# Differential and local attention: products with the values for pairs of query blocks

## The chip, the core and the metric

The kernel runs on one NeuronCore of a Trainium2 chip. The metric is the device time of one execution, in microseconds (us), from runs without the profiler; a further, profiled execution gives the trace from which all rows below are taken. TensorE multiplies matrices (in the profile PE; the loading of its stationary operand is PEld), VectorE is DVE, ScalarE is ACT, GpSimd is POOL, and SyncE (SP) issues most loads.

## The reference

Two transformer-like blocks follow each other on a sequence of 1024 positions and width 1024, all in float32. The change touches the attention of the second block. Cut to what matters:

```python
# local (sliding window) attention: 8 heads, a block of 128 queries sees its own and the block before
scores = q_block @ [k_prev, k_own].T * d**-0.5 - slope * delta          # masked, window 128
p      = softmax([scores, sink])[..., :-1]
out_a  = p @ [v_prev, v_own]                                            # 256 keys -> 64 columns
# differential attention: 4 heads of two maps, causal, a block of 128 queries sees all keys before it
p      = softmax(q_m @ k_m.T * d**-0.5 - slope * delta)                 # m = 0, 1
out_d  = (p_0 - lam * p_1) @ v                                          # up to 1024 keys -> 128 columns
out_d  = rmsnorm(out_d, subln_g) * 0.8                                  # over the 128 columns of a head
merged = sigmoid(ga) * (out_a @ w_branch_swa) + sigmoid(gd) * (out_d @ w_branch_diff)
x      = x + gate1 * (merged @ w_out)
```

## The kernel before

The sequence is worked on in two halves of 512 columns. Projections (`proj`, tile `pj`) keep activations transposed and split every operand into a high and a low part, so that a product is three TensorE rows of 512 columns (`wh` with both parts of the activation, `wl` with the high part). They are emitted in a fixed order by `run_...()` calls. Everything else is a generator, a side task: attention units, norms, sums. The class `Sched` holds an estimated clock for each engine and decides, before each projection row, which side task's next rows are emitted ahead of it; `Sched.note` has the estimated duration of each operation. So the order on each engine is settled when the kernel is built. Where a projection needs what a side task makes, `sch.until(...)` emits side tasks' rows alone until a flag is set. The body is built twice, the first time to learn when tiles come free.

`swa` (L1233) is the local attention: a unit `(t, n)` has two heads and one block of 128 queries; scores go into one bank (`z`), the softmax is in tile `p`, `turn(p, 4)` transposes its four 128x128 blocks on TensorE (`tr`) and copies them on ScalarE into `pT` (`aT` in the trace), and the products with the values go into a bank `o` of four query blocks. Two heads write partitions 0 to 63 and 64 to 127 of it.

`diff` (L1314) is the differential attention. A unit `(h, i)` is a head and a block of queries with `n = i + 1` blocks of keys. `softmax` runs for both maps in turn: scores `z`, one or two VectorE passes that add the bias and take the maximum, the exponential on ScalarE, a scaling on VectorE. Then `p0` is turned, and `n` products of one 128x128 block of `v` (`vp`, stationary) with 128 columns of `aT` are summed in `o`. When a head's four blocks are done, `sub_norm` squares, sums (`sm`), spreads the factor (`rb`), scales, and splits the result into the activation `od` that the branch projection `job_br` reads. All of these products are plain float32; each stands in the trace as two PE records and two PEld records.

`crew` keeps at most `width` units alive (2 in the second half, `PACE`). `fetched` issues the loads of the next head on SP as soon as `room(tiles + KEEP)` finds that many of the 34 large tiles free (`N4`, `in_use`); `work` asks `room` for its own large tiles. A block with more than 512 keys needs three large ones (two maps, one turned), a shorter one none.

The second half of `diff` is to be done when `run_br1` (the branch projection) starts:

```python
        run_g1()
        run_up0()
        sch.until(lambda: ("attn2", 1) in flags)
        run_br1()
```

Of the kernel before, what the change touches and what calls it, by code (L numbers as in the profile page):

```python
# [18 lines left out]
HT = 512  # L19
# [38 lines left out]
class Sched:  # L58
# [94 lines left out]
    def note(self, eng, op, out, args, extra=0.0):  # L153
        ready = self.ready
        names = [a.tensor.name for a in args]
        self.seq += 1
        start = max([self.clk[eng]] + [ready.get(n, 0.0) for n in names])
        o = out.tensor.name
        n = out.free_size()
        lat = 0.1  # L160
        if eng == "pe":
            start = max(start, self.fresh.pop(o, 0.0))
            if op == "transpose":
                d = 0.113 if self.t > 30.0 else 0.213
            elif args[0].dtype == F32R:
                d = n / 2400 if n >= 256 else n / 600
            elif args[0].dtype == BF16:
                d = n / 2400
            elif n == 1:
                d = 0.2 if self.t > 30.0 else 0.37  # L170
            else:
                d = n / 600 if args[0].free_size() == 128 else n / 1070
            d += 0.0026
        elif eng == "act":
            d = n / 1400 + 0.155 + extra
        elif eng == "dve":
            fast = op in ("tensor_scalar", "tensor_copy") and all(a.space == out.space != bass.MemoryType.PSUM
                                                                  for a in args)
            d = n / (1920 if fast else 960) + 0.06
            if op == "reciprocal":  # L180
                d += n / 192
        else:
            d = 1.05 if eng == "pool" else 0.55
            nbytes = n * out.shape[0] * 4
            t = max(self.clk["dma"], start + d) + nbytes / 360e3
            self.clk["dma"] = t
            lat = t + 1.8 - start - d
        self.clk[eng] = start + d
        for nme in names + [o]:
            self.last[nme] = self.seq, max(start + d + lat, self.last.get(nme, (0, 0.0))[1])  # L190
        ready[o] = max(ready.get(o, 0.0), start + d + lat) if eng != "pe" else start + d + lat
        if eng != "pe":
            for nme in names:
                b = self.in_bank.get(nme)
                if b is not None:
                    b[0] = max(b[0] or 0.0, start + d)
# [68 lines left out]
def tile_body(  # L265
# [14 lines left out]
    sch = Sched()  # L280
# [3 lines left out]
    mm = ten.matmul  # L284
# [12 lines left out]
    out = out[0]  # L297
# [10 lines left out]
    def free(n=1):  # L308

        in_use[0] -= n  # L310

    def room(n, hold=0):

        while in_use[0] + n > N4:
            yield 0.4
        in_use[0] += hold

    def big(shape, dt=F32, name="b", held=False):
        in_use[0] += not held
        return s4.tile([128] + shape, dt, nm(name))  # L320

    def sml(w=HT, dt=F32, name="s"):
        return s2.tile([128, w], dt, nm(name))
# [4 lines left out]
    def bank(name="ps"):  # L328
        return sch.new_bank(lambda n: pp.tile([128, HT], F32, tag=f"bk{n}", name=nm(name)))
# [679 lines left out]
    def turn(src, n):  # L1009

        dst = wide(n * 128, name="aT", held=True)
        for b0 in range(0, n, 4):
            b1 = min(n, b0 + 4)
            yield from sch.a_bank()
            ps = bank("tr")
            for b in range(b0, b1):
                ten.transpose(out=ps[:, (b - b0) * 128:(b - b0 + 1) * 128],
                              in_=src[:, b * 128:(b + 1) * 128], identity=ident)
            sca.copy(out=dst[:, b0 * 128:b1 * 128], in_=ps[:, 0:(b1 - b0) * 128])
        yield dst  # L1020
        return dst

    def fetched(loads, keys, need, fetch, tiles, ahead=1):

        for n, key in enumerate(keys):
            while (need(key) not in flags) or (n > ahead and keys[n - ahead - 1] not in loads["done"]):
                yield 0.5
            yield from room(tiles + (KEEP if n else 0))
            loads[key] = fetch(key)
# [203 lines left out]
    def swa(live, half, width, rho):  # L1233
# [15 lines left out]
        def work(t, n):  # L1249
# [32 lines left out]
                vec.tensor_scalar(out=p[:, 256 * h:256 * h + 256], in0=p[:, 256 * h:256 * h + 256],  # L1282
                                  scalar1=l[:, h:h + 1], scalar2=None, op0=ALU.mult)
            yield p
            pT = yield from turn(p, 4)
            if t not in st:
                yield from sch.a_bank()
            if t not in st:
                st[t] = [bank("o"), 0]
            po = st[t][0]  # L1290
            g = t // 2
            blocks = [(0, n - 1), (1, n)] if n else [(0, 0)]
            for a, (b, kb) in enumerate(blocks):
                for h in range(2):
                    mm(po[64 * h:64 * h + 64, (n % 4) * 128:(n % 4 + 1) * 128],
                       lhsT=vas[0][:, kb, 64 * g:64 * g + 64],
                       rhs=pT[:, (2 * h + b) * 128:(2 * h + b + 1) * 128],
                       start=a == 0, stop=a == len(blocks) - 1)
            st[t][1] += 1
            if st[t][1] == 4:  # L1300
                del loads[t], st[t]
                loads["done"].add(t)
# [11 lines left out]
    def diff(live, half, width, rho):  # L1314
# [43 lines left out]
        def work(h, i):  # L1358
            yield from arrived(loads, h)
            n = i + 1  # L1360
            w = n * 128
            yield from room(3 * (w > HT), 3 * (w > HT))
            p0, l0 = yield from softmax(h, i, 0)
            vec.tensor_scalar(out=p0[:, 0:w], in0=p0[:, 0:w], scalar1=l0[:, 0:1], scalar2=None, op0=ALU.mult)
            p1, l1 = yield from softmax(h, i, 1)
            vec.scalar_tensor_tensor(out=p0[:, 0:w], in0=p1[:, 0:w], scalar=l1[:, 0:1], in1=p0[:, 0:w],
                                     op0=ALU.mult, op1=ALU.add)
            free(w > HT)
            fr = st.setdefault(("f", h), set())
            fr.add(i)  # L1370
            if len(fr) == 4:
                del loads[h]
                loads["done"].add(h)
                free(3 + half)
            yield p0
            aT = yield from turn(p0, n)
            free(w > HT)
            if h not in st:
                yield from sch.a_bank()
            if h not in st:  # L1380
                st[h] = [bank("o"), 0]
            po = st[h][0]
            vt = vts[h]
            yield vt
            for kb in range(n):
                mm(po[:, (i % 4) * 128:(i % 4 + 1) * 128], lhsT=vt[:, kb * 128:(kb + 1) * 128],
                   rhs=aT[:, kb * 128:(kb + 1) * 128], start=kb == 0, stop=kb == n - 1)
            free(w > HT)
            st[h][1] += 1
            if st[h][1] == 4:  # L1390
                del st[h], vts[h]
                free(half)
                o = sml(name="od")
                sca.copy(out=o, in_=po)
                sq = sml(name="sq")
                act(out=sq, in_=po, func=ACTF.Square)
                sch.spawn(sub_norm(h, o, sq))
# [936 lines left out]
```

## Time and profile before

| | |
|---|---|
| median of 3 runs | 2580.68 us (2580.65 to 2581.55) |
| the profiled execution's own time | 2582.41 us, its span 2580.6 us |
| TensorE (PE) busy | 2505.5 us, 97% of the span |
| its granted clock, mean over the span | 0.991 of full speed |
| VectorE, ScalarE, GpSimd busy | 69%, 49%, 19% of the span |

The span is the time between the first and the last instruction. Busy time counts records that overlap once. The granted clock is the share of TensorE's full speed (2.4 GHz) that the throttle allowed; it has two levels, full and half.

### The profile page before, as it was taken

To read this page: it belongs to the slowest core of one execution; us is meant where nothing else is said; L and a number is where in the kernel's file an instruction comes from. 1 tells how busy PE (TensorE), PEld (TensorE's weight loads), DVE (VectorE), ACT (ScalarE), POOL (GpSimd) and SP (SyncE) were. 2 spreads that over 40 slices of the span, in tenths; PEclk is the share of its full clock that TensorE was granted. 3 is DMA by queue.
4 is the path that set the end of the run, shared out by engine and by line. 5 is a ranking of instruction groups with operands and counts; after the bars stand their busy time and mean duration, and the time that the engine had idled before them with its cause. 6 is when DMAs were issued, how large, how long until landed. Compare 5 with 4: busy or idle time off the path is not lost.

```text
span 2580.6 us, 38805 instructions
## 1 busy us (share of the span) xinstructions
PE 2505.5 (97%) x13215; PEld 2057.5 (80%) x13215; DVE 1792.8 (69%) x3245; ACT 1255.7 (49%) x2529; POOL 490.0 (19%) x894
## 2 busy tenths in 40 slices
PE   7999999989999899998999999999999899999998
PEld 6888888879877677787888887888888678788887
DVE  7866666777697788986765556774666876677555
ACT  5311112555455677677664353564634634345442
POOL 0012112312101002331211321222222222221000
PEclk9999999999999999999999999999999999999999
DMA  9867869857897665775876978977886987978764
GB/s 283 264 190 201 203 214 280 235 185 249 279 274 222 204 163 157 221 192 140 250 217 160 262 209 261 260 226 220 200 237 217 237 225 235 238 225 252 226 201 130
DMA packets 541726, 570.43 MB, mean 221 GB/s; under 512 B 32910, under 2 KB 410008, under 8 KB 541528
## 3 DMA queue, kind: packets, MB, share of 16 engines
q1 hardware_dynamic: 482644, 381.99, 50.3%
q0 software_dynamic: 56528, 181.75, 25.3%
q10 hardware_dynamic: 2356, 4.21, 0.4%
q8 instruction: 104, 1.70, 0.3%
q14 instruction: 94, 0.77, 0.1%
HBM read 466.90 MB, written 186.91 MB: 253 GB/s over the span
## 4 chain that ended last, share of the span: by engine, by line
PE 65%; DVE 5%; DMA 3%; ACT 2%; issue 2%; SPq 0%; POOL 0%; DVEq 0%; ACTq 0%; POOLq 0%
PE pj L249 53%; PE o L249 4%; PE z L249 4%; PE tr L250 3%; DVE om L250 2%; PE pv L249 1%; DMA wr<-sg_d2g 1%; DVE be L250 1%; DVE wl L250 1%; DMA wr<-in_b_w_out_dram 1%; DVE ob L250 1%; DVE act L250 0%; DVE fa L250 0%; ACT om L250 0%; ACT be L250 0%
## 5 line engine op out<-in xcount | busy, mean ns | idle before, releaser
L249 PE MATMUL pj<-act,wh 128*128 128x512 f32 (+1 forms) x5680 | 1783.0, 395 | 26.2 <-DVE act L250 16.8
L249 PEld LDWEIGHTS pj<-act,wh 128*128 128x128 f32 x5680 | 1046.2, 189 | 256.8 <-DVE act L250 22.9
L249 PE MATMUL pj<-act,wl 128*128 128x512 f32 (+1 forms) x2840 | 1113.7, 392 | 0.0
L249 PEld LDWEIGHTS pj<-act,wl 128*128 128x128 f32 x2840 | 536.2, 189 | 123.1 <-DVE wl L250 1.3
L250 DVE TENSOR_TENSOR wl<-wr,wh 128x512 fp32r<-128x512 f32 x714 | 476.4, 679 | 169.7 <-ACT wh L250 156.2
L250 ACT CAST wh<-wr 128x512 fp32r<-128x512 f32 x714 | 425.8, 617 | 177.6 <-PE pj L249 41.8
L250 POOL COPY paced<-wl 128x1 f32<-128x1 f32 x256 | 114.7, 448 | 881.6 <-DVE wl L250 840.9
L250 ACT COPY aT<-tr 128x512 f32<-128x512 f32 (+3 forms) x272 | 128.7, 501 | 162.0 <-PE tr L250 159.6
L249 PE MATMUL z<-kd,qs 128*128 128x512 f32 (+2 forms) x704 | 166.4, 350 | 1.7 <-DVE o L250 0.7
L250 DVE SCALAR_TENSOR_TENSOR acc<-mw,silu_c,acc 128x512 f32<-128x512 f32 x196 | 146.5, 748 | 2.7 <-DMA mw<-in_a_mod_w_dram 0.3
L249 PEld LDWEIGHTS z<-kd,qs 128*128 128x128 f32 x704 | 113.7, 190 | 19.4 <-issue 7.2
L250 DVE TENSOR_TENSOR_SCAN om<-om,begin 128x640 f32<-128x640 f32 (+3 forms) x64 | 120.6, 1885 | 10.2 <-ACT om L250 10.2
L249 PEld LDWEIGHTS o<-aT,vp 128*64 128x64 f32 (+2 forms) x1440 | 99.9, 149 | 22.8 <-issue 14.5
L249 PE MATMUL o<-aT,vp 128*64 128x128 f32 (+2 forms) x1440 | 116.3, 280 | 0.4 <-ACT aT L250 0.4
L250 ACT COPY u<-pj 128x512 f32<-128x512 f32 x46 | 27.0, 588 | 157.8 <-PE pj L249 80.1
L250 ACT ACTIVATE p<-p,t 128x256 f32<-128x256 f32 (+7 forms) x128 | 81.3, 636 | 20.7 <-DVE t L250 20.5
L250 ACT ACTIVATE sq<-xn 128x512 f32<-128x512 f32 x48 | 30.6, 637 | 110.6 <-DVE xn L250 110.5
L250 ACT ACTIVATE om<-z 128x384 f32<-128x384 f32 (+2 forms) x128 | 69.3, 542 | 22.6 <-PE z L249 19.0
L249 PE MATMUL pj<-wh,act 128*128 128x256 f32 x448 | 79.9, 281 | 0.0
L250 PE MATMUL tr<-ident,be 128*128 128x128 f32 x416 | 61.1, 283 | 18.1 <-DVE be L250 17.7
L250 PEld LDWEIGHTS tr<-ident,be 128*128 128x128 f32 x416 | 47.3, 143 | 32.4 <-DVE be L250 20.7
L250 DVE TENSOR_TENSOR be<-be,om 128x639 f32<-128x639 f32 (+3 forms) x64 | 66.2, 1034 | 6.7 <-ACT sq L250 0.5
(252 smaller groups left out, 2757.5 us busy)
## 6 DMA issues: line engine op xcount, KB each, us to landing
wr<-in_w_in_dram SPq DMA_DIRECT2D x136, 256.0 KB
mw<-in_w_ada_dram SPq DMA_DIRECT2D x96, 256.0 KB
wr<-in_a_w_in_dram SPq DMA_DIRECT2D x80, 256.0 KB
al<-dn_d SPq DMA_DIRECT2D x77, 256.0 KB
wr<-in_w_up_dram SPq DMA_DIRECT2D x66, 256.0 KB
sw_d<-in_w_down_dram POOLq DMA_DIRECT2D x48, 352.0 KB, 5.0
wr<-in_b_w_qz_dram SPq DMA_DIRECT2D x64, 256.0 KB
qs<-q_d SPq DMA_DIRECT2D x64, 256.0 KB
```

The costliest lines, as they stand in the source:

```text
L249: return f(out, *value, **kw)
L250: return f(out=out, **kw)
```

## The change

A unit no longer multiplies by itself. In `diff`, blocks `i0` and `i0 + 1` share turned tiles in which 256 columns stand for each block of keys, 128 of either query block (`pair_new`, `turn_pair`). The unit that ends second multiplies for both: each key block of `v` is loaded once and 256 columns pass it; the last key block, which only the odd query block sees, gets 128. The large tiles of a pair (one or two) are asked for by the even unit and given back after the products. In `swa`, the pair's turned blocks share one large tile `pT`; the key block that both query blocks see gets 256 columns, its two neighbours 128. The planner's estimate for float32 products is changed too: before, 128 columns at 600 per us (1070 with 64 stationary columns); now, 1100 per us and at least 0.213 us (2200 and 0.108).

```diff
             elif n == 1:
                 d = 0.2 if self.t > 30.0 else 0.37
             else:
-                d = n / 600 if args[0].free_size() == 128 else n / 1070
+                d = max(n / 1100, 0.213) if args[0].free_size() == 128 else max(n / 2200, 0.108)
             d += 0.0026
         elif eng == "act":
             d = n / 1400 + 0.155 + extra
@@ -1019,6 +1019,30 @@
             sca.copy(out=dst[:, b0 * 128:b1 * 128], in_=ps[:, 0:(b1 - b0) * 128])
         yield dst
         return dst
+
+    def pair_tiles(i):
+
+        return (i % 8) // 2 if i < 4 else 2
+
+    def pair_new(i):
+        return [sml(name="aT")] if i == 0 else [big([2 * HT], name="aT", held=True) for _ in range(pair_tiles(i))]
+
+    def pair_block(tiles, kb, j):
+
+        return tiles[kb // 4][:, kb % 4 * 256 + 128 * j:kb % 4 * 256 + 256]
+
+    def turn_pair(src, n, tiles, j):
+
+        for b0 in range(0, n, 4):
+            b1 = min(n, b0 + 4)
+            yield from sch.a_bank()
+            ps = bank("tr")
+            for b in range(b0, b1):
+                ten.transpose(out=ps[:, (b - b0) * 128:(b - b0 + 1) * 128],
+                              in_=src[:, b * 128:(b + 1) * 128], identity=ident)
+            dst = tiles[b0 // 4].rearrange("p (k j q) -> p k j q", j=2, q=128)
+            sca.copy(out=dst[:, 0:b1 - b0, j, :], in_=ps[:, 0:(b1 - b0) * 128].rearrange("p (k q) -> p k q", q=128))
+        yield tiles
 
     def fetched(loads, keys, need, fetch, tiles, ahead=1):
 
@@ -1282,21 +1306,37 @@
                 vec.tensor_scalar(out=p[:, 256 * h:256 * h + 256], in0=p[:, 256 * h:256 * h + 256],
                                   scalar1=l[:, h:h + 1], scalar2=None, op0=ALU.mult)
             yield p
-            pT = yield from turn(p, 4)
+            n0, j = n & ~1, n % 2
+            if (t, n0) not in st:
+                yield from room(1)
+            if (t, n0) not in st:
+                st[t, n0] = [big([2, HT], name="aT"), []]
+            pT, done = st[t, n0]
+            yield from sch.a_bank()
+            ps = bank("tr")
+            for b in range(4):
+                ten.transpose(out=ps[:, b * 128:(b + 1) * 128], in_=p[:, b * 128:(b + 1) * 128], identity=ident)
+            sca.copy(out=pT[:, :, 256 * j:256 * j + 256], in_=ps.rearrange("p (h c) -> p h c", h=2))
+            yield pT
+            done.append(j)
+            if len(done) < 2:
+                return
             if t not in st:
                 yield from sch.a_bank()
             if t not in st:
                 st[t] = [bank("o"), 0]
             po = st[t][0]
             g = t // 2
-            blocks = [(0, n - 1), (1, n)] if n else [(0, 0)]
-            for a, (b, kb) in enumerate(blocks):
+
+            runs = [(n0, 1, 0, 2), (n0 - 1, 0, 0, 1), (n0 + 1, 3, 1, 1)] if n0 else [(0, 0, 0, 1), (0, 2, 1, 1), (1, 3, 1, 1)]
+            for a, (kb, c, q0, nq) in enumerate(runs):
                 for h in range(2):
-                    mm(po[64 * h:64 * h + 64, (n % 4) * 128:(n % 4 + 1) * 128],
-                       lhsT=vas[0][:, kb, 64 * g:64 * g + 64],
-                       rhs=pT[:, (2 * h + b) * 128:(2 * h + b + 1) * 128],
-                       start=a == 0, stop=a == len(blocks) - 1)
-            st[t][1] += 1
+                    mm(po[64 * h:64 * h + 64, (n0 % 4 + q0) * 128:(n0 % 4 + q0 + nq) * 128],
+                       lhsT=vas[0][:, kb, 64 * g:64 * g + 64], rhs=pT[:, h, c * 128:(c + nq) * 128],
+                       start=a == 0 or (n0 == 0 and a == 1), stop=a == 2 or n0 + a == 0)
+            del st[t, n0]
+            free()
+            st[t][1] += 2
             if st[t][1] == 4:
                 del loads[t], st[t]
                 loads["done"].add(t)
@@ -1359,7 +1399,13 @@
             yield from arrived(loads, h)
             n = i + 1
             w = n * 128
-            yield from room(3 * (w > HT), 3 * (w > HT))
+            i0, j = i & ~1, i % 2
+            extra = 2 * (w > HT) + (0 if j else pair_tiles(i))
+            while j and (h, i0) not in st:
+                yield 0.4
+            yield from room(extra, extra)
+            if not j:
+                st[h, i0] = []
             p0, l0 = yield from softmax(h, i, 0)
             vec.tensor_scalar(out=p0[:, 0:w], in0=p0[:, 0:w], scalar1=l0[:, 0:1], scalar2=None, op0=ALU.mult)
             p1, l1 = yield from softmax(h, i, 1)
@@ -1373,8 +1419,15 @@
                 loads["done"].add(h)
                 free(3 + half)
             yield p0
-            aT = yield from turn(p0, n)
+            aT = st[h, i0]
+            if not aT:
+                aT.extend(pair_new(i0))
+            yield from turn_pair(p0, n, aT, j)
             free(w > HT)
+            done = st.setdefault((h, i0, "n"), [])
+            done.append(j)
+            if len(done) < 2:
+                return
             if h not in st:
                 yield from sch.a_bank()
             if h not in st:
@@ -1382,11 +1435,13 @@
             po = st[h][0]
             vt = vts[h]
             yield vt
-            for kb in range(n):
-                mm(po[:, (i % 4) * 128:(i % 4 + 1) * 128], lhsT=vt[:, kb * 128:(kb + 1) * 128],
-                   rhs=aT[:, kb * 128:(kb + 1) * 128], start=kb == 0, stop=kb == n - 1)
-            free(w > HT)
-            st[h][1] += 1
+            del st[h, i0], st[h, i0, "n"]
+            for kb in range(i0 + 2):
+                j0 = int(kb > i0)
+                mm(po[:, (i0 % 4 + j0) * 128:(i0 % 4 + 2) * 128], lhsT=vt[:, kb * 128:(kb + 1) * 128],
+                   rhs=pair_block(aT, kb, j0), start=kb == 0, stop=kb > i0)
+            free(pair_tiles(i0))
+            st[h][1] += 2
             if st[h][1] == 4:
                 del st[h], vts[h]
                 free(half)
```

The scheduler orders the rows anew. From the first place that differs, in the first block's attention, on the order differs in many places; from the first row of `run_br1` to the end TensorE's rows are the same, row for row (3121 matmuls). Three places matter below. In the names, `act` is a split activation, `wh` and `wl` the parts of a weight, `z` scores, `tr` a transposition, `sm` and `rb` the norm of `sub_norm`, the number is the tile's.

TensorE, the last head of the second half, up to `run_br1`. Before, its last products and its norm stand among projection rows (the last rows ahead of `run_br1` are shown, then its first four, of tile `pj_19433`):

```order
L249 MATMUL pj_19328<-act_18405,wl_19333 128x512
L249 MATMUL pj_19328<-act_18407,wh_19296 128x512 x2
L249 MATMUL pj_19328<-act_18407,wl_19333 128x512
L249 MATMUL pj_19328<-act_18409,wh_19296 128x512 x2
L249 MATMUL pj_19328<-act_18409,wl_19333 128x512
L250 MATMUL rb_19410<-ident,t_19402 128x128 x4
L249 MATMUL pj_19328<-act_18411,wh_19296 128x512 x2
L249 MATMUL pj_19328<-act_18411,wl_19333 128x512
L249 MATMUL pj_19433<-act_15863,wh_19331 128x512 x2
L249 MATMUL pj_19433<-act_15863,wl_19365 128x512
L249 MATMUL pj_19433<-act_16096,wh_19331 128x512 x2
L249 MATMUL pj_19433<-act_16096,wl_19365 128x512
```

In the change the last projection row ahead of `run_br1` comes earlier, and behind it stand the head's scores, transpositions and products alone; the first rows of that stretch are

```order
L249 MATMUL pj_18947<-act_17965,wh_18911 128x512 x2
L249 MATMUL pj_18947<-act_17965,wl_18952 128x512
L250 MATMUL sm_19096<-ident,sq_19064 128x128 x4
L249 MATMUL z_19120<-kd_18403,qs_18407 128x384 x2
L250 MATMUL tr_19126<-ident,p_19011 128x128 x4
L249 MATMUL z_19132<-kd_18403,qs_18407 128x384 x2
L250 MATMUL tr_19136<-ident,p_19011 128x128
L249 MATMUL z_19150<-kd_18402,qs_18406 128x512 x2
L249 MATMUL z_19154<-kd_18402,qs_18406 128x384 x2
L250 MATMUL rb_19158<-ident,t_19144 128x128 x4
L250 MATMUL tr_19173<-ident,p_19080 128x128 x4
L250 MATMUL tr_19181<-ident,p_19080 128x128 x2
```

and its last rows, with the first of `run_br1`, are

```order
L250 MATMUL tr_19244<-ident,p_19149 128x128 x3
L250 MATMUL tr_19256<-ident,p_19208 128x128 x4
L250 MATMUL tr_19262<-ident,p_19208 128x128 x4
L249 MATMUL o_19197<-aT_19232,vp_18400 128x256 x4
L249 MATMUL o_19197<-aT_19233,vp_18400 128x256 x3
L249 MATMUL o_19197<-aT_19233,vp_18400 128x128
L250 MATMUL sm_19283<-ident,sq_19280 128x128 x4
L250 MATMUL rb_19302<-ident,t_19300 128x128 x4
L249 MATMUL pj_19317<-act_15855,wh_18950 128x512 x2
L249 MATMUL pj_19317<-act_15855,wl_18991 128x512
```

What moved: 28 rows of this list (76 matmuls: 20 `z`, 26 `tr`, 16 `sm` and `rb`, 14 `o`) now follow each other with no projection row between them: the norm of the head before, and of the last head all transpositions and products, the second map of its second block, both maps of its third and fourth, and its norm.

SP, the loads of `diff`'s third head in the second half (`vp` with 8 blocks, two `kd`, `qs`). Before they follow the second head's by one weight load:

```order
L250 DMA qs_17437<-qd_d 64x2x512 x2
L250 DMA qs_17438<-qd_d 64x2x512 x2
L250 DMA wr_17469<-in_w_in_dram 128x4x128
L250 DMA vp_17497<-vd_d 128x8x128
L250 DMA kd_17499<-kd_d 128x1024
L250 DMA kd_17500<-kd_d 128x1024
L250 DMA qs_17503<-qd_d 64x2x512 x2
L250 DMA qs_17504<-qd_d 64x2x512 x2
L250 DMA wr_17515<-in_w_in_dram 128x4x128
```

In the change they come 38 rows behind the second head's, together with those of the fourth head:

```order
L250 DMA wr_18351<-in_w_up_dram 128x4x128
L250 DMA wr_18370<-in_w_up_dram 128x4x128
L250 DMA vp_18388<-vd_d 128x8x128
L250 DMA kd_18390<-kd_d 128x1024
L250 DMA kd_18391<-kd_d 128x1024
L250 DMA qs_18394<-qd_d 64x2x512 x2
L250 DMA qs_18395<-qd_d 64x2x512 x2
L250 DMA vp_18400<-vd_d 128x8x128
L250 DMA kd_18402<-kd_d 128x1024
L250 DMA kd_18403<-kd_d 128x1024
L250 DMA qs_18406<-qd_d 64x2x512 x2
L250 DMA qs_18407<-qd_d 64x2x512 x2
L250 DMA wr_18415<-in_w_up_dram 128x4x128
```

What moved: the third head starts later, the fourth at about its old place.

TensorE, the end of `diff`'s first half (head 3, the last products, `sm`, `rb`). Before, projection rows stand between the last products and `sm`, and between `sm` and `rb`:

```order
L249 MATMUL o_13929<-aT_14070,vp_13559 128x128 x4
L249 MATMUL pj_14082<-act_10691,wh_13948 128x512 x2
L249 MATMUL pj_14082<-act_10691,wl_14001 128x512
L249 MATMUL pj_14082<-act_10724,wh_13948 128x512 x2
L249 MATMUL pj_14082<-act_10724,wl_14001 128x512
L249 MATMUL pj_14082<-act_10767,wh_13999 128x512 x2
L249 MATMUL pj_14082<-act_10767,wl_14039 128x512
L249 MATMUL pj_14082<-act_10783,wh_13999 128x512 x2
L249 MATMUL pj_14082<-act_10783,wl_14039 128x512
L250 MATMUL sm_14125<-ident,sq_14103 128x128 x4
L249 MATMUL pj_14082<-act_10838,wh_13999 128x512 x2
L249 MATMUL pj_14082<-act_10838,wl_14039 128x512
```

In the change the last transposition, the products and `sm` follow each other directly, and `rb` comes after six projection matmuls:

```order
L249 MATMUL pj_14086<-act_10754,wl_14032 128x512
L250 MATMUL tr_14167<-ident,p_14078 128x128 x4
L249 MATMUL o_14106<-aT_14109,vp_13670 128x256 x3
L249 MATMUL o_14106<-aT_14109,vp_13670 128x128
L250 MATMUL sm_14195<-ident,sq_14186 128x128 x4
L249 MATMUL pj_14160<-act_14190,wh_14030 128x512 x2
L249 MATMUL pj_14160<-act_14190,wl_14091 128x512
L249 MATMUL pj_14160<-act_9577,wh_14030 128x512 x2
L249 MATMUL pj_14160<-act_9577,wl_14091 128x512
L250 MATMUL rb_14235<-ident,t_14218 128x128 x4
L249 MATMUL pj_14160<-act_14220,wh_14030 128x512 x2
```

What moved: the projection rows that stood between these steps.

## Rows read from the trace of the kernel before

**Rows 1.** The page: TensorE's busy time, and its granted clock in 40 slices.

```profile
PE 2505.5 (97%) x13215; PEld 2057.5 (80%) x13215; DVE 1792.8 (69%) x3245; ACT 1255.7 (49%) x2529; POOL 490.0 (19%) x894
PEclk9999999999999999999999999999999999999999
```

**Rows 2.** By form: count | busy us, mean ns | idle before.

```profile
L249 PE MATMUL o<-aT,vp 128*128 128x128 f32 x288 | 37.0, 275 | 0.0
...
L250 PE MATMUL vt<-ident,rows 95*128 95x95 f32 x1 | 0.2, 245 | 0.0
L250 PE MATMUL vt<-ident,rows 66*128 66x66 f32 x1 | 0.2, 221 | 0.0
```

**Rows 3.** Timeline of TensorE, differential attention: start us, us, what.

```profile
1854.02 1.95 PE L249 MATMUL o<-aT,vp 128*128 128x128 f32 x16
1855.72 0.71 PE L249 MATMUL pj<-act,wh 128*128 128x512 f32 x2
```

**Rows 4.** The same, local attention.

```profile
1248.49 0.66 PE L249 MATMUL o<-aT,vas 128*64 128x128 f32 x8
1249.08 0.50 PE L249 MATMUL z<-kd,qs 128*128 128x256 f32 x2
```

**Rows 5.** The same, eight float32 records of one moving column.

```profile
30.48 0.95 PE L249 MATMUL sm<-ones,acc 128*128 128x1 f32 x8
31.29 0.49 PE L249 MATMUL pj<-act,wh 128*128 128x512 f32 x1
```

**Rows 6.** The same, the only float32 product of over 128 columns.

```profile
992.76 0.71 PE L249 MATMUL row<-row,ones 1*128 1x264 f32 x2
993.40 0.44 PE L249 MATMUL o<-aT,vp 128*64 128x128 f32 x4
```

**Rows 7.** Windows: busy us of PE, PEld, DVE, ACT, POOL; granted clock.

```profile
700.00:1160.00 460.00, 437.76 (x2963) 352.28 (x2961) 391.11 (x500) 308.02 (x698) 75.75 (x112) 0.99 0.72 208
1160.00:1350.00 190.00, 182.84 (x1169) 153.59 (x1168) 128.46 (x393) 129.76 (x306) 35.84 (x72) 0.98 0.71 198
...
880.00:890.00 10.00, 4.32 (x17) 3.71 (x18) 9.10 (x10) 6.67 (x18) 1.08 (x2) 0.68 0.75 255
1181.00:1191.00 10.00, 4.99 (x30) 4.29 (x32) 0.77 (x3) 9.94 (x22) 0.00 (x0) 0.82 0.41 106
...
1640.00:1866.00 226.00, 226.00 (x1181) 191.65 (x1180) 145.19 (x346) 129.65 (x232) 55.90 (x110) 1.00 0.79 217
```

**Rows 8.** Windows, tile `p` alone, the last head: PE, PEld, DVE, ACT.

```profile
1802.00:1848.00 46.00, 2.45 (x18) 2.15 (x18) 16.28 (x24) 8.44 (x16) 1.00 0.77 184
```

**Rows 9.** Timeline of TensorE at the end of that head.

```profile
1858.58 0.60 PE L250 MATMUL sm<-ident,sq 128*128 128x128 f32 x4
1858.93 0.71 PE L249 MATMUL pj<-act,wh 128*128 128x512 f32 x2
...
1865.29 0.60 PE L250 MATMUL rb<-ident,t 128*128 128x128 f32 x4
```

**Rows 10.** Groups by form of VectorE and ScalarE, 1640 to 1873 us.

```profile
L250 DVE DVE_READ_ACCUMULATOR2_ANT t<- 128x1 f32 x61 | 5.0, 83 | 0.0
L250 DVE RECIPROCAL t<-t 128x1 f32<-128x1 f32 x32 | 5.0, 157 | 2.9 <-ACT p L250 2.9
...
L250 DVE TENSOR_REDUCE t<-sm 128x4 f32<-128x512 f32 x5 | 3.5, 692 | 9.7 <-PE sm L250 9.7
...
L250 DVE TENSOR_TENSOR fa<-fa,pj 128x512 f32<-128x512 f32 x5 | 3.4, 687 | 13.8 <-ACT fa L250 13.6
...
L250 DVE SCALAR_TENSOR_TENSOR od<-od,g,rb 128x512 f32<-128x512 f32 x4 | 3.0, 747 | 1.4 <-ACT rb L250 1.4
...
L250 ACT ACT_TABLE_LOAD x13 | 16.7, 1283 | 0.2
L250 ACT COPY aT<-tr 128x512 f32<-128x512 f32 x20 | 11.5, 588 | 22.3 <-PE tr L250 22.3
L250 ACT ACTIVATE p<-p,t 128x1024 f32<-128x1024 f32 x8 | 9.2, 1155 | 4.4 <-DVE t L250 4.3
```

## Prediction

> **What bounds the kernel now.** I read the page first. TensorE is busy for 2505.5 of 2580.6 us and its granted clock is at the full level in all 40 slices [rows 1]; VectorE has a third of its time to spare. So a change pays only in two ways: TensorE's rows get shorter, or TensorE waits less. It costs in the same two ways. Next I read windows, to see where TensorE waits in the stages that the change touches. In 700 to 1160 us it is busy 437.8 of 460 us, in 1160 to 1350 us 182.8 of 190 us: some 29 us of idle time [rows 7]. From 1640 to 1866 us, the second half of `diff`, it is busy 226.00 of 226 us [rows 7]. There is nothing to win by waiting less in that last stretch, and any wait put there is paid in full. A VectorE or ScalarE row costs nothing there now, since projection rows lie beside it.
>
> **Price of the products.** Count first. Each float32 product is two records. `diff` has 288 records, so 144 products [rows 2]; a pair with n and n + 1 key blocks had 2n + 1 products and now has n of 256 columns and one of 128. Over four heads that is 144 products before, 64 of 256 and 16 of 128 after. `swa` has 8 heads with 15 products each (one for the first query block, two for each of seven), 120; after it 24 of 256 and 72 of 128. What a product of 128 columns costs is read from starts, since the ends are modelled: 16 records take 1.70 us, 0.106 each [rows 3]; in `swa`, where two heads fill half the columns of the array each, 8 take 0.59 us, 0.074 each [rows 4].
>
> No product of 256 columns stands in the trace, so its price is bounded. If the load of the stationary block sets the pace, 256 columns are as quick as 128. Eight float32 records of one column start 0.81 us apart from first to next product, 0.10 each [rows 5], so a load does take as long as 128 columns do now. Then one of two products is free: 64 x 2 x 0.106 = 13.6 us in `diff` and 24 x 2 x 0.074 = 3.6 us in `swa`, a gain of 17.2 us. If the columns set it, 256 cost what 2 x 128 cost. Two readings say so. A record of 95 columns is given 245 ns, one of 66 221 ns: 24 ns for 29 columns, 0.83 ns for each, and 128 columns with 275 ns lie on the same line [rows 2]; 256 columns need 0.213 us by that, exactly twice 0.106. And the one float32 product of more than 128 columns, of 264, takes 0.64 us from its start to the next product's, with two records [rows 6]; less a load's 0.10 at its start and as much where the next begins, 0.22 each. Two of 128 would be 0.21 with load and all. The other end is to take that 0.64 us whole for 256 columns: 64 x (0.64 - 4 x 0.106) = 14 us lost, and 2 to 3 us more in `swa`. I take the columns' price, where both rows lie, and 0.5 us of gain for fewer starts.
>
> The Trainium skill ("TensorE: Matmul & The Clock Gate", the section on the back-to-back issue gap) has N columns cost N / 2.4 GHz and some 2.5 ns, measured in bf16; as an estimate that is 109 ns for 256 columns, and by it the change would gain about what the load's pace gives. It speaks for the change. "FP8 and Floating Point Precision" in the Trainium skill (TensorE Precision Notes) says that true float32 takes four passes through the array; that speaks against it, and the trace's 0.83 ns for a column in each of two records agrees with it.
>
> **The order, second half of `diff`: the main term.** The even unit of a pair now holds the pair's tiles until the odd one has multiplied. `room` therefore finds tiles free later, and the third head's loads on SP, which came one weight load behind the second's, come 38 rows later, with the fourth's (the lists above). The head then runs late. Before, its `sm` and `rb` start at 1858.58 and 1865.29 us with projection rows directly behind each [rows 9]. After the change 76 matmuls of the last head and the norm of the head before it stand bare ahead of `run_br1`: TensorE has nothing to put between.
>
> How long do they last? TensorE's own rows: 42 transpositions and norm matmuls at 0.09 to 0.11 us (`sm` takes 0.35 for four [rows 9]) are 4.2 us; 20 `z` at 0.19, the mean record of that stretch (226 us by 1181 records [rows 7]), 3.8; 12 `o` products at 2 x 0.213 and two at half that, 5.6: nearly 14 us. The chain they wait on is longer:
> - VectorE on the head. Its 24 passes over `p` are 16.3 us [rows 8]; with them go 16 reads of the maximum at 83 ns, 8 reciprocals and 4 products with lambda at 157 ns [rows 10], 3.2 us, so 19.5. The first block's scores and first scaling lie ahead of the last projection row; they are 15 of the head's 104 passes over one block (52 for scores, 52 for scaling), 2.8 us of the 19.5. Left: 16.7.
> - In the same queue stand a gelu product (0.69), the sum of the norm before (0.69), five small rows (0.8), `od`'s scaling (0.75) and its low part (0.69) [rows 10]: 3.6.
> - VectorE's own waits: at least the last exponential, 1.16 [rows 10], which has nothing behind it to cover it; with up to two table loads at 1.28 on ScalarE, up to 4. I take 2.5.
> - Behind VectorE's last pass: 8 transpositions 0.9, the copy 0.59, the eight last products 3.2, the copy of `o` and its square 1.2 (at the copy's 0.59 each), `sm` 0.35, the sum 0.69, seven small rows 1.1, `rb` 0.35 [rows 9, 10], and eight handovers between engines, about 1 to 1.5: 9.6 to 10.
>
> The sum is 32.5 (31 to 37), less TensorE's 14: about **19 us idle** (17 to 23). Nothing gives this back later: from the first row of `run_br1` TensorE's order is the same to the end, and that part is bound by TensorE. Idle TensorE also drops to its lower clock here: in 10 us in which it was busy for 4.3, the granted clock was 0.68, in another with 5.0 busy, 0.82 [rows 7]. If the 14 us of rows run in part at half speed and the first rows behind too, that is 1 to 6 us: **+4**.
>
> **The end of the first half.** There the last transposition, the products and `sm` now touch, and `rb` follows after six matmuls. The copies (0.59 for `aT`; 1.2 for `o` and its square [rows 10]) and the chain from `sm` to `rb` (0.69 + 1.1, less the 1.3 that six matmuls cover) come bare: 0.6 + 1.2 + 1.0 with handovers, **+3** (0 to 6).
>
> **SP, POOL, the wait in the loop.** The polling of the odd unit for the even one happens while the kernel is built and emits nothing. The late loads pass weight loads on SP; those keep their place before the projections that read them, and TensorE's stretch is full without them. ScalarE's copies write 128-column pieces with a stride; nothing in the trace prices that, and projections hide them up to the tail. I take 0 (0 to 1).
>
> **The sum**, against the profiled execution's 2582.4 us: -0.5 + 19 + 4 + 3 = +25.5, so 2607.9. The median of the runs lies 1.7 us below the profiled one: **2606 us**.
>
> **Rivals.**
> - *Columns are free* (the load's pace holds): -17 in place of -0.5, 2589.5 us, 2581 to 2595. The pace of [rows 5] speaks for it, [rows 2, 6] against. It would be no loss only if the tail came under some 13 us. Chance 0.10.
> - *The reorder repairs the waits ahead* (the other side). The planner's new estimates shuffle rows from the first block's attention on. Of the 29 us of idle time in 700 to 1350 us, 20 or more would have to go, for the result to be within 0.2% or better: 2606 - 20 = 2586, at best 2577. Against it: around 880 us VectorE is busy 9.1 of 10 us [rows 7], and VectorE's work there is not made less. Chance 0.07.
> - *The reorder adds waits ahead*, or the tail's ScalarE rows (copies, exponentials and table loads in turn) come in series with VectorE's: 5 us from the tail's upper end, 5 to 15 from stretches such as that at 1181 us, where ScalarE is the bound (9.9 of 10 us [rows 7]): 2616 to 2630. Chance 0.15.
> - *Forecast*, 2595 to 2616: 0.68.
>
> A change within 0.2%, 5.2 us, is about what a measurement of this kernel can't tell from none. Faster needs two of the favourable cases together, 0.03; the same, 0.06; slower, 0.91. For 8 in 10 the range takes in the upper half of the free columns' case and the lower part of the added waits: 2588 to 2620.
>
> **What will show it.** `o` records of 256 columns start 0.21 us apart; at 0.11 the price is wrong and 17 us come back. Just ahead of `run_br1`, TensorE is idle for some 19 us, VectorE is busy for most of that stretch, the released waits are `tr` on `p`, and the granted clock falls under 1. If it runs full there, the main term is wrong. From `run_br1` to the end the length is that of before; if it differs, the wait is paid back or grows.

## The result: 1.1% slower, and the profile after

The changed kernel takes 2609.61 us (2605.54 to 2615.11, 4 runs) against 2581.11 us before: ratio 1.0107, 95% interval 1.0081 to 1.0132. Its profiled execution took 2606.89 us, with a span of 2605.0 us, 24.4 us more than that of before. Predicted were 2606 us, 2588 to 2620. The page's busy times and clock (answering to [rows 1]):

```profile
PE 2508.7 (96%) x13039; PEld 2058.4 (79%) x13039; DVE 1793.0 (69%) x3245; ACT 1258.4 (48%) x2532; POOL 490.7 (19%) x894
PEclk9999999999999999999999999999899999999999
```

TensorE has 176 records fewer (two for each of 64 and 24 products) and is busy for 3 us more. One slice of the clock has dropped. The windows of the second half (answering to [rows 7]; busy us of PE, PEld, DVE, ACT, POOL, then the granted clock) show where:

```profile
1640.00:1844.00 204.00, 204.00 (x964) 169.81 (x963) 119.66 (x274) 109.98 (x197) 49.47 (x100) 1.00 0.83 230
1844.00:1881.00 37.00, 21.38 (x94) 17.15 (x93) 20.89 (x61) 20.84 (x34) 6.13 (x13) 0.80 0.47 103
1881.00:1891.00 10.00, 10.00 (x40) 8.11 (x39) 6.21 (x10) 4.26 (x8) 2.06 (x4) 0.87 0.47 112
1891.00:2036.00 145.00, 145.00 (x631) 117.58 (x630) 92.86 (x155) 63.58 (x109) 40.85 (x72) 1.00 0.77 224
```

Up to 1844 us TensorE is as full as before. Then come 37 us in which it is busy for 21.4 at a mean granted clock of 0.80, and 10 more at 0.87. The timeline of TensorE in that stretch (start, us, what, and in brackets the idle time before it with its releaser):

```profile
1844.51 0.60 PE L250 MATMUL sm<-ident,sq 128*128 128x128 f32 x4
1844.87 0.59 PE L249 MATMUL z<-kd,qs 128*128 128x384 f32 x2
1849.37 1.10 PE L250 MATMUL tr<-ident,p 128*128 128x128 f32 x4 [3.91 <-DVE p L250]
...
1855.56 0.89 PE L250 MATMUL tr<-ident,p 128*128 128x128 f32 x6 [2.15 <-DVE p L250]
...
1864.95 0.63 PE L250 MATMUL tr<-ident,p 128*128 128x128 f32 x4 [2.31 <-DVE t L250]
...
1870.22 1.97 PE L250 MATMUL tr<-ident,p 128*128 128x128 f32 x8 [3.84 <-DVE p L250]
1872.01 4.13 PE L249 MATMUL o<-aT,vp 128*128 128x256 f32 x16
1877.32 0.66 PE L250 MATMUL sm<-ident,sq 128*128 128x128 f32 x4 [1.18 <-ACT sq L250]
1880.21 1.11 PE L250 MATMUL rb<-ident,t 128*128 128x128 f32 x4 [2.23 <-DVE t L250]
1880.98 1.20 PE L249 MATMUL pj<-act,wh 128*128 128x512 f32 x2
```

These are the 28 rows of the list in the section on the change: 36.5 us from the first `sm` to the first row of `run_br1`, six waits of 15.6 us together. In four of them `tr` waits for VectorE (three times the profile names `p`, once `t`); the last two are the norm's, `sm` for the square and `rb` for the sum and its small rows. The load of `vp` for the third head, which the prediction made the cause, is issued at 1752.85 us here and at 1663.00 us before (timelines of SP, first before, then after):

```profile
1663.00 0.54 SPq L250 DMA_DIRECT2D vp<-vd_d  x1
```

```profile
1752.85 0.54 SPq L250 DMA_DIRECT2D vp<-vd_d  x1
```

To see where all of the 24.4 us went I take the start of the same projection record in both traces, at places up to which TensorE has done the same work (the products with the values apart, where they are paired). The differences between such places, in us, for this trace and those of the experiments (each against the trace of before, whose times head the columns):

| | to 736 | to 1110 | to 1363 | to 1618 | to 1873 | to 2036 | to 2277 | to 2524 | sum |
|---|---|---|---|---|---|---|---|---|---|
| the change | +2.6 | -3.0 | -4.0 | -1.6 | **+21.8** | -0.3 | **+7.6** | +1.3 | +24.4 |
| again | +2.6 | -0.1 | -4.2 | -1.6 | +23.6 | -0.3 | +8.8 | +1.5 | +30.4 |
| split | +1.9 | -0.8 | -5.6 | -1.5 | +23.5 | -0.3 | +7.1 | +1.5 | +25.7 |
| keep5 | -0.3 | +1.1 | -3.8 | -1.6 | -1.1 | +0.1 | +3.2 | +2.5 | +0.1 |
| keep6 | +3.0 | -0.2 | -3.8 | -1.6 | -1.0 | 0.0 | +0.8 | +1.5 | -1.2 |
| late | +2.5 | -3.8 | -4.1 | -1.6 | -1.5 | -0.1 | -4.4 | +3.6 | -9.3 |
| bkeep9 | +3.5 | -0.9 | -0.1 | 0.0 | +29.0 | -0.1 | -4.0 | +0.2 | +27.5 |
| bnote | +0.4 | -3.1 | -4.4 | +0.3 | +6.5 | -0.2 | -3.9 | +0.9 | -3.4 |
| swakeep5 | -0.6 | -2.0 | -6.4 | -1.6 | -0.2 | 0.0 | +0.9 | +1.4 | -8.5 |
| diffkeep5 | -0.6 | -2.4 | -1.7 | -0.4 | -0.6 | -0.1 | +11.9 | +1.0 | +7.0 |
| latenote | -0.2 | -1.9 | -2.3 | -2.1 | +4.9 | -0.2 | -1.3 | +2.6 | -0.7 |

The first two columns are mostly chance of one execution: the change and its repeat are the same program and differ by 2.9 us in the second, and bkeep9, whose rows are those of before up to the second half, stands at +3.5 in the first.

### The profile page after: what moved, and what is told of

It is laid out like the page before. It is cut to its first block, busy times and chain, and to the rows that moved or that the text cites. A ratio compares the mean times of both kernels' runs of the same rounds, so it can differ in the third digit from the quotient of the medians.

```text
span 2605.0 us, 38442 instructions
## 1 busy us (share of the span) xinstructions
PE 2508.7 (96%) x13039; PEld 2058.4 (79%) x13039; DVE 1793.0 (69%) x3245; ACT 1258.4 (48%) x2532; POOL 490.7 (19%) x894
## 4 chain that ended last, share of the span: by engine, by line
PE 64%; DVE 7%; DMA 2%; ACT 2%; issue 2%; POOL 0%; SPq 0%; DVEq 0%; ACTq 0%; POOLq 0%
PE pj L249 51%; PE o L249 4%; PE z L249 4%; PE tr L250 3%; DVE om L250 2%; PE pv L249 2%; DMA wr<-sg_d0g 1%; DVE fa L250 1%; DVE wl L250 1%; DVE be L250 1%; DVE act L250 1%; DMA wr<-sg_d2g 1%; DVE t L250 0%; ACT L250 0%; DMA dn_d<-fa 0%
## 5 line engine op out<-in xcount | busy, mean ns | idle before, releaser
L249 PEld LDWEIGHTS o<-aT,vp 128*64 128x64 f32 (+2 forms) x1312 | 93.0, 144 | 26.1 <-issue 14.4
L249 PE MATMUL o<-aT,vp 128*64 128x128 f32 (+3 forms) x1312 | 112.7, 289 | 0.9 <-ACT aT L250 0.9
L250 PE MATMUL tr<-ident,be 128*128 128x128 f32 x416 | 61.5, 283 | 16.7 <-DVE be L250 12.7
L250 DVE TENSOR_REDUCE t<-sm 128x4 f32<-128x512 f32 x40 | 27.6, 689 | 64.7 <-PE sm L250 64.7
```

Source lines behind the costliest of these rows:

```text
L249: return f(out, *value, **kw)
L250: return f(out=out, **kw)
```

## The experiments

**again: the change once more.**

> The changed kernel once more, for a second trace beside the first. Theory A (the rows of the last head, bare ahead of run_br1, cost some 22 us; the order after run_br1 costs another 8; the order ahead of the last head gains some 10): ratio 1.009 to 1.012, TensorE idle 15 to 17 us in the stretch ahead of run_br1, and again 7 to 8 us more idle than before between 2100 and 2320 us. Theory B (those 8 us and the first 3 us were chance of one execution): the idle time ahead of run_br1 is the same, the other two differ from the first trace.

Ratio 1.011 (1.0095 to 1.0124). The stall ahead of `run_br1` stands again, with 15.4 us of waits. So do the 8 us behind 2036 us, though only 5.4 of them are idle time of TensorE (18.4 us against 13.0); neither is chance of an execution. Of the gain ahead of 1700 us (8.6 us in the first trace up to 1618, from 736) 5.9 are left.

**split: the price alone.** Pairs, tiles and the order of every other row stay; a pair's products go past `v` twice, 128 columns each time:

```diff
-            for kb in range(i0 + 2):
-                j0 = int(kb > i0)
-                mm(po[:, (i0 % 4 + j0) * 128:(i0 % 4 + 2) * 128], lhsT=vt[:, kb * 128:(kb + 1) * 128],
-                   rhs=pair_block(aT, kb, j0), start=kb == 0, stop=kb > i0)
+            for q in range(2):
+                for kb in range(i0 + 1 + q):
+                    mm(po[:, (i0 % 4 + q) * 128:(i0 % 4 + q + 1) * 128], lhsT=vt[:, kb * 128:(kb + 1) * 128],
+                       rhs=pair_block(aT, kb, q)[:, 0:128], start=kb == 0, stop=kb == i0 + q)
```

(`swa` likewise; the lines that keep the planner's charge the same are left out here.) 

> The change with its pairing, tiles and order kept on every engine, but each product of 256 columns given as two of 128 (88 products instead of 64 and 24; the planner is charged the same). Theory A (the columns set the price, 0.216 us for a record of 256): within 3 us of the changed kernel, o records of 128 columns 0.106 to 0.112 apart, diff's products 31 to 33 us in sum by either form. Theory B (256 columns save the load): slower than the changed kernel by some 17 us.

Ratio 1.0095 (1.0082 to 1.0108), within the interval of the change's two. The same products in both timelines, first of the change (14 records of 256 columns and 2 of 128), then of this run (30 of 128):

```profile
1839.30 3.40 PE L249 MATMUL o<-aT,vp 128*128 128x256 f32 x16
1842.46 1.52 PE L249 MATMUL z<-kd,qs 128*128 128x384 f32 x8
```

```profile
1839.60 3.51 PE L250 MATMUL o<-aT,vp 128*128 128x128 f32 x30
1842.87 1.55 PE L250 MATMUL z<-kd,qs 128*128 128x384 f32 x8
```

3.16 us against 3.27: 0.21 us for a record of 256 columns, 0.109 for one of 128. Of 30 loads 14 are saved, and 0.1 us in 3.3 with them. Theory B is out.

In `swa` pairing does shorten the products, but not by saving loads. A group of 8 records takes 0.59 us before [rows 4], two of them 1.18; the pair's 12 records take 1.02 us from 1518.86 us in the change, and the 16 records of 128 columns in this run 1.02 us from 1518.69 us. Over the whole kernel, from start to next start and without idle time, they take 18.2 us before, 15.4 in the change and 15.5 here. What the change and this run have in common is that a pair's products stand in one group instead of two.

**keep5 and keep6: one tile.** In `diff`'s second half `fetched` asks for 5 or 6 large tiles beyond a head's own 5, instead of `KEEP` = 7:

```diff
-            yield from room(tiles + (KEEP if n else 0))
+            yield from room(tiles + (keep if n else 0))
...
-        sch.spawn(fetched(loads, range(4), lambda h: ("qd", h, half), fetch, 3 + 2 * half))
+        sch.spawn(fetched(loads, range(4), lambda h: ("qd", h, half), fetch, 3 + 2 * half, keep=6 if half else KEEP))
```

> The change, but in diff's second half the loads of the next head want 5 large tiles to spare instead of 7. The rows up to the second half keep their order; the third head's loads come 350 projection matmuls earlier, and no list of more than 14 matmuls stands bare ahead of run_br1. Theory A (the tail's stall comes from the late loads of a head, by way of the pair's tiles): the 15 to 17 us of idle ahead of run_br1 and the half-clock rows go, time 2584 to 2590 us. Theory B (the head ends late because its chain is longer, or VectorE is behind at the end in any case): a stall of 10 us or more remains, 2598 to 2608 us.

> The change with 6 large tiles to spare instead of 7 for the loads of diff's next head in the second half: one tile less. The third head's loads then come 290 projection matmuls earlier, the fourth's 90, and no list of more than 14 matmuls stands bare ahead of run_br1. Theory A (one tile decides on the stall): TensorE idle for less than 1 us ahead of run_br1, within 0.5% of before. Theory B (two tiles at least are missing, or the stall has another cause): ratio 1.006 or more, as the change.

keep5: ratio 1.0001 (0.9992 to 1.0009), 2583.58 us. keep6: 0.9978 (0.9969 to 0.9987), faster than before. In keep6 the third head's `vp` is issued at 1661.22 us. The window of keep6 up to `run_br1`:

```profile
1640.00:1862.00 222.00, 221.88 (x1070) 185.25 (x1069) 143.24 (x341) 124.69 (x228) 51.60 (x104) 1.00 0.78 217
```

TensorE waits for 0.12 us where the change waits for 15.6. A single tile decides on the whole stall. With `KEEP` the loads want 12 of 34 tiles free, with 6 they want 11: since 11 are enough to let the third head in and 12 are not, it was one tile that it missed its moment by.

**late: the even unit holds no tile for the pair before the turn.**

```diff
-            extra = 2 * (w > HT) + (0 if j else pair_tiles(i))
+            extra = 2 * (w > HT)
...
-            aT = st[h, i0]
-            if not aT:
-                aT.extend(pair_new(i0))
+            if (h, i0, "t") not in st:
+                st[h, i0, "t"] = 1
+                yield from room(pair_tiles(i0), pair_tiles(i0))
+                st[h, i0].extend(pair_new(i0))
+            while not st[h, i0]:
+                yield 0.4
+            aT = st[h, i0]
```

(A line that removes the new flag is left out.)

> The change, but a pair's large tiles are asked for when the first of its two blocks is to be turned, not at the start of the even unit. Third head's loads as in keep5, the fourth's as in the change. Theory A (tiles held by the even unit delay the loads): as keep5, 2584 to 2590 us. Theory B (the tiles are as scarce while the turned blocks wait for the odd unit, or the end is late in any case): 2598 to 2608 us.

Ratio 0.9975 (0.9966 to 0.9984), 2577.19 us: below what Theory A gave, the third head's `vp` issued at 1658.62 us, the stall gone, and 4.4 us gained from 2036 to 2277 us instead of 7.6 lost.

**bkeep9: the stall without the change.** The kernel before, with `keep=9` in the second half as the only edit.

> The kernel before with one number changed: in diff's second half the loads of the next head want 9 large tiles to spare instead of 7. Nothing is paired, the products keep 128 columns; up to the first loads concerned the rows keep their order. The third and the fourth head's loads come 320 and 250 projection matmuls later, and 123 matmuls stand bare ahead of run_br1. Theory A (late loads of a head make the stall): 18 to 30 us slower than before, TensorE idle for 15 us or more ahead of run_br1 with tr waiting on p. Theory B (the stall comes from the pairing): within 5 us of before.

Ratio 1.0095 (1.0081 to 1.0109), 23 us at the medians. The third head's `vp` is issued at 1762.23 us. TensorE's waits ahead of `run_br1` are of the kind of the change's, 17.7 us together:

```profile
1850.98 2.05 PE L249 MATMUL o<-aT,vp 128*128 128x128 f32 x16 [0.24 <-ACT aT L250]
1854.38 0.66 PE L250 MATMUL sm<-ident,sq 128*128 128x128 f32 x4 [1.35 <-ACT sq L250]
1857.38 1.08 PE L250 MATMUL rb<-ident,t 128*128 128x128 f32 x4 [2.34 <-DVE t L250]
...
1867.88 2.86 PE L250 MATMUL tr<-ident,p 128*128 128x128 f32 x11 [4.73 <-DVE p L250]
...
1883.54 3.56 PE L250 MATMUL tr<-ident,p 128*128 128x128 f32 x15 [5.57 <-DVE p L250]
...
1891.68 0.66 PE L250 MATMUL sm<-ident,sq 128*128 128x128 f32 x4 [1.23 <-ACT sq L250]
1894.57 1.11 PE L250 MATMUL rb<-ident,t 128*128 128x128 f32 x4 [2.23 <-DVE t L250]
```

Late loads alone are enough for the stall; no product was paired here.

**bnote, swakeep5, diffkeep5, latenote: whose is the gain ahead?** bnote is the kernel before with the new line of `note`; swakeep5 and diffkeep5 take the change for one of the two attentions with keep5's edit; latenote is late with the old line of `note`.

> The kernel before with the change's estimates for the planner and nothing else: no pairing. Theory A (the 8 to 10 us gained ahead of the last head come from the new order that the estimates give): some 8 us ahead at equal work at 1700 us, ratio 0.996 to 0.999. Theory B (they come from the pairing): within 3 us of before there, ratio 0.999 to 1.002.

> Pairs in swa alone, diff as before, the new estimates, and 5 large tiles to spare in diff's second half, so that no stall stands ahead of run_br1. Theory A (order by the estimates): the same gain of some 8 us at 1700 us as in the change. Theory B (pairing of swa): a gain between 1160 and 1640 us alone, 3 to 6 us. Against before 0.996 to 1.001.

> Pairs in diff alone, swa as before, the new estimates, and 5 large tiles to spare in diff's second half. Theory A (order by the estimates): the same gain of some 8 us at 1700 us as in the change. Theory B (pairing of swa): none of it. Behind run_br1 the loss of 6 to 10 us that the change, its repeat and the version with 5 tiles to spare show: if it is bound to diff's pairing it is there, and absent where swa alone is paired. Against before 0.997 to 1.002.

> The pairing with a pair's tiles asked for at the turn, as in the run that did so before, but with the planner's old estimates. TensorE's rows, the products apart, are those of before up to the last products of swa's second query pairs. Theory A (the gain of some 8 us ahead of 1360 us comes from the order that the new estimates give, none from the pairing): at equal work within 2 us of before at 1110 and 1360 us, and the gain of the earlier run is gone; 5 us of bare rows ahead of run_br1 cost some 6. Ratio 1.000 to 1.004. Theory B (pairing gives it): 5 us or more ahead at 1360 us, ratio 0.997 to 1.000.

Ratios: bnote 0.9993 (0.9983 to 1.0002), swakeep5 0.9975 (0.9966 to 0.9984), diffkeep5 1.0037 (1.0025 to 1.005), latenote 1.0008 (1.0000 to 1.0017). Neither theory holds whole. From 1110 to 1363 us bnote gains 4.4 us without any pair and the change 4.0, so the new estimates alone are enough for that gain. But latenote gains 2.3 there with pairs and the old estimates, and diffkeep5 only 1.7 with the new ones: it hangs on the order that each version gets, and no single part is shown to make it. From 1363 to 1618 us every version that pairs `swa` gains 1.5 to 2.1 us, bnote and bkeep9 none and diffkeep5 0.4: that goes with the pairing of `swa`. Since split gains 1.5 there without a product of 256 columns, it does not come from saved loads. (bnote and latenote lose 6.5 and 4.9 us ahead of `run_br1`, where 5 us of rows stand bare in their order too.) Behind 2036 us diffkeep5 loses 11.9 us, but late, with the same pairs in `diff`, gains 4.4: the loss there is not bound to `diff`'s pairing, against what the expectation of diffkeep5 set up.

## Why the prediction was right, step by step

**Price of the products: right for the record, too small a gain in the sum.** Predicted 0.213 us for a record of 256 columns and 0.5 us of gain; measured 0.21, and 0.1 us in a set of 3.3. The gain that was missed is `swa`'s 2.8 us, which split has too and which the prediction did not look for. By the gap that the Trainium skill gives for a matmul by itself ("TensorE: Matmul & The Clock Gate", the section on the back-to-back issue gap) a record of 256 columns would have been an estimated 109 ns; for these float32 records the trace shows twice that, so a rule that was measured in another type must be checked against a row of the type at hand. By the same rule 128 columns are an estimated 56 ns, so it makes 256 cost about as much as 2 x 128; the prediction read a gain out of it by setting 109 ns beside the 0.106 us of the trace, which mixes the two.

**The tail: right in place, cause and sum; its parts less so.** Predicted 19 us of idle time and 4 of clock, 23 in all; measured 15.6 us idle, and in all 21.8 us in the change and 23.6 in its repeat. The half clock took more than I gave it: TensorE's rows ran at it for 10.6 us in the stretch and 2.5 us behind it, an estimated 6.6 us lost (half of that time). So the idle time was put too high and the clock too low, and the two misses nearly cancel. TensorE's rows filled 20.9 us where 14 were reckoned; an estimated 5.3 of these are the half clock. VectorE's work came as reckoned: 16.7 + 3.6 us in the sum, busy for 20.9 of 37 us in the trace. Its idle time came longer, 16 us of the 36.5 where 2.5 waiting and 9.7 at the end were reckoned. One wait is on TensorE, whose order puts products ahead of its next scores (timeline of all engines):

```profile
1857.74 3.49 PE L249 MATMUL o<-aT,vp 128*128 128x256 f32 x12
...
1860.99 1.65 PE L249 MATMUL z<-kd,qs 128*128 128x512 f32 x6
1861.75 0.69 DVE L250 CUSTOM_DVE_ANT_0 p<-z,DD 128x512 f32<-128x512 f32 x1 [2.33 <-PE z L249]
```

For 2.3 us the vector work stands behind twelve records of products, which themselves run in part at half clock. keep6, late and bkeep9 show the cause from three sides: a head's loads that come late make the stall, and a tile that the even unit holds made them late.

**The end of the first half: two of three waits as forecast, of no weight in the sum.** After the change:

```profile
1341.10 0.66 PE L250 MATMUL tr<-ident,p 128*128 128x128 f32 x4
1342.69 1.78 PE L249 MATMUL o<-aT,vp 128*128 128x256 f32 x8 [0.94 <-ACT aT L250]
1345.71 0.65 PE L250 MATMUL sm<-ident,sq 128*128 128x128 f32 x4 [1.23 <-ACT sq L250]
...
1348.58 0.80 PE L249 MATMUL pj<-act,wh 128*128 128x512 f32 x1 [1.87 <-DVE act L250]
```

The first two stand where they were forecast and are new, 2.2 us together (1.8 predicted for them). The third is a projection, not `rb`, and it is not new: before, that row and the one ahead of it wait for 1.93 us.

```profile
1353.82 0.50 PE L249 MATMUL pj<-act,wh 128*128 128x512 f32 x1 [1.71 <-ACT act L250]
1354.55 0.70 PE L249 MATMUL pj<-act,wh 128*128 128x512 f32 x1 [0.22 <-DVE act L250]
```

So some 2 us came of the 3 predicted. Yet the stretch from 1110 to 1363 us as a whole came out 4.0 us shorter. Of these only 0.7 are idle time that went (10.5 to 9.8 us); some 1.6 are `swa`'s products, and the rest is not traced to single rows.

**"From `run_br1` to the end the length is that of before": wrong.** From 1873 us, 6.7 us behind its first row, to the end it is 8.6 us longer here and 10.0 in the repeat, at the same order of TensorE. The same stretch of work, 2036 to 2277 us in the trace of before, first before, then after (windows, columns as above):

```profile
2036.20:2277.00 240.80, 227.79 (x951) 180.07 (x950) 167.91 (x289) 100.02 (x173) 63.95 (x124) 0.97 0.84 225
```

```profile
2051.80:2300.10 248.30, 228.90 (x951) 180.28 (x950) 168.09 (x289) 100.68 (x173) 66.63 (x127) 0.97 0.83 220
```

All engines do nearly the same work; TensorE waits 19.4 us instead of 13. In the timeline its new waits end with rows of ScalarE or VectorE; that these free a bank late is my reading and not shown. Three of them:

```profile
2137.31 0.74 PE L249 MATMUL pj<-act,wh 128*128 128x512 f32 x2 [2.09 <-ACT v L250]
...
2169.38 0.74 PE L249 MATMUL pj<-act,wh 128*128 128x512 f32 x2 [1.14 <-DVE y L250]
...
2199.44 0.73 PE L249 MATMUL pj<-act,wh 128*128 128x512 f32 x2 [1.98 <-DVE y L250]
```

VectorE's, ScalarE's and GpSimd's rows do stand in another order there. The stall by itself is not the cause (bkeep9 has it and gains 4.0 us there), nor is the pairing by itself (late). What in that order makes the waits stays open.

So the sum, +25.5 predicted and +24.4 in the trace, was met in part by luck. The trace's sum is 2.6 us lost up to 736 us (chance of an execution), 8.6 gained from there to 1618 us (5.9 in the repeat), where I had 3 lost, 21.8 lost in the tail, and 8.6 lost behind 1873 us, where I had none. The gain ahead and the loss behind are misses against each other. The rival in which the reorder repairs waits came true for a small part only: from 736 to 1363 us TensorE's idle time fell by 2.3 us, from 30.2 to 27.9.

## What to carry to other kernels

Sharing a load paid nothing in `diff`, since the columns set the pace of its products: find a row with other column counts in the same type before counting saved loads. Where a planner grants loads by free buffers, one buffer held longer can push a prefetch past its moment and cost a stall many times its own worth; ask how close the grant was, and let a shared buffer be taken at its first write. Asking for the pair's tiles at the turn, or wanting one tile less to spare, turns 1.1% slower into 0.2% faster. `diff`'s pairing has no share in that gain that a run shows: swakeep5, which pairs `swa` alone, has the same ratio of 0.9975 as late.

## What was not expected of the hardware

The clock's share. The 36.5 us of the tail held waits of 15.6 us, none longer than 3.9, and the granted clock of the stretch was 0.80. It fell to half four times: at 1849.4 and 1856.2 us just behind waits of 3.91 and 2.15 us, at 1866.5 and 1880.1 us within waits of 3.84 and 2.23 us. At the end it stayed at half for 2.5 us of gapless work and then was full (windows, columns as above):

```profile
1881.00:1883.50 2.50, 2.50 (x8) 2.01 (x7) 0.77 (x2) 1.25 (x3) 0.00 (x0) 0.50 0.00 0
1883.60:1891.00 7.40, 7.40 (x33) 6.01 (x32) 5.34 (x9) 2.91 (x6) 2.06 (x4) 1.00 0.64 151
```

So waits of 15.6 us cost an estimated 6.6 us more by the clock (half of the 10.6 and 2.5 us in which rows ran at it).
